# Feed-forward of a two-layer diffusion trunk: gate and up rows by Strassen's seven products, g through HBM, all output products at the end

## The chip, the cores and the metric

One core of one Trainium2 chip runs the whole program in one launch. The metric is the device time of that launch in microseconds (us). Engines are named as in the profile: PE is TensorE's matmuls and PEld its weight loads, DVE is VectorE, ACT is ScalarE, POOL is GpSimd, SP is SyncE, whose queue issues the DMAs.

## What is computed

Two layers over 256 context tokens and 512 latent tokens of width 1024. Each layer is a feed-forward, an attention and a second feed-forward, so there are four feed-forwards, called FFN 0 to FFN 3 here. The last one, FFN 3, has only the 512 latent tokens. What matters of the reference:

```python
def swiglu(h, w_in, w_out):              # w_in (1024, 2 * 2816), w_out (2816, 1024)
    gate, up = jnp.split(h @ w_in, 2, axis=-1)
    return (jax.nn.silu(gate) * up) @ w_out

def half_ffn(h, m, k, g_pre, g_post, w_in, w_out):
    y = swiglu(modulated_norm(h, g_pre, m, k), w_in, w_out)
    return gated_residual(h, y, g_post, m, k, 0.5)
```

## The kernel before

All products are made of fp32r matmuls on split operands: a number x is kept as a high half (a cast to fp32r) and a low half (x minus that), and a product takes three matmuls, high by high, high by low, low by high. `split` (L103) makes the halves: ACT casts (L104) and DVE subtracts (L105). `load_w` loads a weight block of 128 by 1024 into one of four `stage` buffers and splits it into one of six `wh` and six `wl` buffers.

The normed, transposed tokens are the moving operand u, split into `uh` and `ul`: 512 tokens in one tile and 256 in another, each with 8 blocks k of 128 features. `split_u` writes them, DVE and POOL sharing the low half of some tiles (L298, L299).

`ffn` (L424) goes over 22 chunks of 128 hidden features. `w_in` makes gate and up rows of a chunk: two weight blocks, 8 blocks k, 3 matmuls, each over 512 and over 256 tokens (L447): 96 matmuls, or 48 of 512 columns in FFN 3. Then ACT takes silu of gate (L490), DVE multiplies by up to g (L491), casts and subtracts (L501, L502), and g stays on the chip as the stationary operand of the output products. `w_out` adds the output products of a part (pairs of chunks, and six at the end) to `ys`, a tile of 128 tokens at a time, half a row of 1024 at a time (`project_half`, L404; `add_y`, L395). Parts follow each other so that the `w_in` of the next chunk stands in front of the `w_out` of the last part. The first chunk (two of them in FFN 3) runs over pairs of token tiles, 256 columns at a time, since the tokens come in tile by tile from the sub-layer before.

With the last part goes `Finish`: for each token tile the gate multiply on POOL (L350), the norm, the residual (L363), the next norm (L369), transposes on PE (L263), modulation (L277, L273) and the split. In that part the order of DVE, ACT and POOL is the program's (`ordered`); elsewhere in a feed-forward a planner that simulates the engines lays the instructions of every engine out at build time, by priority and by what it holds ready.

Between the products `Fillers` run steps of the conditioning vectors (`ada`): 6, 4, 5 and 1 vectors in FFN 0 to 3, ten steps each, of which eight load 128 by 1024 of weights into a `stage` buffer and make two DVE multiply-adds of 1024 columns (L169, L173).

## Time and profile before

| what | value |
|---|---|
| median of 3 runs | 2843.75 us (2843.62 to 2847.32) |
| the profiled execution: span from first to last instruction | 2845.6 us |
| PE busy | 2766.2 us, 97% |
| DVE busy | 1703.9 us, 60% |
| ACT busy | 908.6 us, 32% |
| POOL busy | 357.7 us, 13% |
| DMA | 291.71 MB, queues 32.3% of 16 engines' span |

A matmul's own duration in the profile is its latency; matmuls are pipelined, so what one costs in a stream is the distance from one start to the next. A group's mean is over all its instructions. "idle before" is the idle time of the engine ahead of an instruction, with what ended it.

### The profile page before, as it was taken

To read this page: it belongs to the slowest core of one execution; us is meant where nothing else is said; L and a number is where in the kernel's file an instruction comes from. 1 tells how busy PE (TensorE), PEld (TensorE's weight loads), DVE (VectorE), ACT (ScalarE), POOL (GpSimd) and SP (SyncE) were. 2 spreads that over 40 slices of the span, in tenths; PEclk is the share of its full clock that TensorE was granted. 3 is DMA by queue.
4 is the path that set the end of the run, shared out by engine and by line. 5 is a ranking of instruction groups with operands and counts; after the bars stand their busy time and mean duration, and the time that the engine had idled before them with its cause. 6 is when DMAs were issued, how large, how long until landed. Compare 5 with 4: busy or idle time off the path is not lost. (4 is left out here: it accounts for less than half of the span.)

```text
span 2845.6 us, 38736 instructions
## 1 busy us (share of the span) xinstructions
PE 2766.2 (97%) x15472; PEld 2399.3 (84%) x15472; DVE 1703.9 (60%) x2516; ACT 908.6 (32%) x1887; POOL 357.7 (13%) x645
## 2 busy tenths in 40 slices
PE   7999999989999989999999999999999899899998
PEld 5888888879999978888888888888888899788887
DVE  5657565367777787456544475556544778755543
ACT  4211111146665564211111232111113554632221
POOL 0000000054333342000000210000002410200001
PEclk9999999999999999999999999999999999999999
DMA  7534334231111115233232243334422211243332
GB/s 239 172 94 146 114 118 136 74 111 44 36 37 41 53 67 174 83 111 122 83 106 89 97 158 104 108 100 128 122 89 97 97 46 53 88 146 111 111 119 74
DMA packets 276812, 291.71 MB, mean 103 GB/s; under 512 B 13032, under 2 KB 231320, under 8 KB 276632
## 3 DMA queue, kind: packets, MB, share of 16 engines
q1 hardware_dynamic: 276632, 289.24, 32.3%
q8 instruction: 121, 1.98, 0.3%
q14 instruction: 59, 0.48, 0.1%
HBM read 272.38 MB, written 16.83 MB: 102 GB/s over the span
## 5 line engine op out<-in xcount | busy, mean ns | idle before, releaser
L447 PE MATMUL ff_ps<-uh,wl 128*128 128x512 f32 (+1 forms) x2544 | 707.8, 342 | 4.2 <-DVE wl L105 4.2
L447 PE MATMUL ff_ps<-uh,wh 128*128 128x512 f32 (+1 forms) x2544 | 704.0, 341 | 5.4 <-ACT uh L1401 3.9
L104 ACT CAST wh<-stage 128x1024 fp32r<-128x1024 f32 x276 | 287.3, 1053 | 1318.1 <-PE ff_ps L447 786.3
L447 PE MATMUL ff_ps<-ul,wh 128*128 128x512 f32 (+1 forms) x2544 | 704.7, 341 | 2.5 <-DVE ul L1402 1.3
L105 DVE TENSOR_TENSOR wl<-stage,wh 128x1024 fp32r<-128x1024 f32 x276 | 333.4, 1220 | 301.2 <-ACT wh L104 301.0
L447 PEld LDWEIGHTS ff_ps<-uh,wh 128*128 128x128 f32 x2544 | 412.0, 189 | 73.0 <-ACT uh L1401 4.0
L447 PEld LDWEIGHTS ff_ps<-uh,wl 128*128 128x128 f32 x2544 | 410.2, 189 | 61.9 <-DVE wl L105 4.6
L447 PEld LDWEIGHTS ff_ps<-ul,wh 128*128 128x128 f32 x2544 | 407.3, 189 | 61.1 <-DVE ul L301 1.8
L395 DVE TENSOR_TENSOR y<-y_ps,y 128x512 f32<-128x512 f32 x412 | 279.7, 688 | 154.3 <-PE y_ps L404 153.2
L404 PE MATMUL y_ps<-wh,g 128*128 128x512 f32 x880 | 344.7, 392 | 0.0
L173 DVE SCALAR_TENSOR_TENSOR acc<-stage,scond,acc 128x1024 f32<-128x1024 f32 x224 | 277.3, 1279 | 50.0 <-DMA stage<-in_ada_w 49.9
L350 POOL TENSOR_TENSOR yg<-y,g 128x512 f32<-128x512 f32 x44 | 57.6, 1309 | 1922.9 <-DVE y L395 1922.9
L491 DVE TENSOR_TENSOR g<-ff_ps,sil 128x768 f32<-128x768 f32 (+2 forms) x89 | 78.4, 881 | 324.4 <-PE ff_ps L447 324.3
L404 PEld LDWEIGHTS y_ps<-wh,g 128*128 128x128 f32 x880 | 165.2, 188 | 36.2 <-DVE y L395 1.6
L404 PE MATMUL y_ps<-wl,g 128*128 128x512 f32 x440 | 171.4, 390 | 0.0
L404 PE MATMUL y_ps<-wl,gh 128*128 128x512 f32 x440 | 171.3, 389 | 0.0
L404 PE MATMUL y_ps<-wh,gh 128*128 128x512 f32 x440 | 171.3, 389 | 0.0
L404 PE MATMUL y_ps<-wh,gl 128*128 128x512 f32 x440 | 171.3, 389 | 0.0
L577 PE MATMUL qkv_ps<-wh,uh 128*128 128x384 f32 x384 | 136.2, 355 | 1.2 <-DVE v L674 1.2
L577 PE MATMUL qkv_ps<-wh,ul 128*128 128x384 f32 x384 | 129.1, 336 | 0.1
L577 PE MATMUL qkv_ps<-wl,uh 128*128 128x384 f32 x384 | 128.8, 335 | 0.0
L404 PE MATMUL y_ps<-wh,ot 128*128 128x512 f32 x320 | 116.2, 415 | 1.2 <-DVE ot L859 0.7
(200 smaller groups left out, 3906.0 us busy)
## 6 DMA issues: line engine op xcount, KB each, us to landing
stage<-in_ffn_w_in SPq DMA_DIRECT2D x176, 512.0 KB
stage<-in_ada_w SPq DMA_DIRECT2D x136, 512.0 KB
stage<-in_ffn_w_out SPq DMA_DIRECT2D x88, 512.0 KB
stage<-in_da_w_in SPq DMA_DIRECT2D x64, 192.0 KB
hd<-h SPq DMA_DIRECT2D x18, 512.0 KB
h<-hd SPq DMA_DIRECT2D x16, 512.0 KB
g<-gd SPq DMA_DIRECT2D x12, 512.0 KB
wl<-hd SPq DMA_DIRECT2D x10, 512.0 KB
```

The costliest lines, as they stand in the source:

```text
L104: nc.scalar.copy(hi, src)
L105: nc.vector.tensor_tensor(out=lo, in0=src, in1=raw(hi), op=ALU.subtract)
L173: nc.vector.scalar_tensor_tensor(out=acc[c], in0=st, scalar=scond[:, k, c : c + 1], in1=acc[c], op0=ALU.mult, op1=ALU.add)
L350: nc.gpsimd.tensor_tensor(out=self.yg[:, cols], in0=ys[t][:, cols], in1=self.gate[1 if t < CT else 0][:, cols], op=ALU.mult)
L395: nc.vector.tensor_tensor(out=y, in0=ps, in1=y, op=ALU.add)
L404: nc.tensor.matmul(ps, lhsT=x, rhs=w, start=(i == 0), stop=(i == n - 1))
L447: nc.tensor.matmul(ps[:, o : o + m], lhsT=ww[:, k, :], rhs=uu[i][:, k, c0 : c0 + m], start=(k == 0 and n == 0), stop=(k == KC - 1 and n == 2),
L491: nc.vector.tensor_tensor(out=of(g), in0=up, in1=of(sil), op=ALU.mult)
L577: nc.tensor.matmul(ps[:, :n], lhsT=x, rhs=w, start=(k == 0 and m == 0), stop=(k == KC - 1 and m == 2))
```

## The change

The tokens are laid out as two halves of 384 (256 in FFN 3): `uh` and `ul` become one tile of (half, k, token) each. A chunk's product [gate; up] by u is taken as a 2 by 2 by 2 block product: gate and up rows, the lower and upper 512 features, the two token halves. It is made of seven products (the form of Strassen's scheme with few additions), each 4 blocks k, 3 matmuls, 384 columns: 84 matmuls a chunk. The first chunk (the first two in FFN 3) stays as it was.

Once per feed-forward, behind the last split of u, four sums of u's blocks are made in `ys` and split. Per chunk, four sums of weight blocks are made on POOL and seven half blocks are split; the sums that undo the scheme are on DVE and POOL. The g of every chunk is stored to HBM. When all chunks are done, g is loaded back in groups, split, and the output products of groups of 2, 3, 3, 3, 3, 3 and 5 chunks follow each other. `operands`, `product`, `chunk`, `operand` and `w_out` are new or rewritten:

```diff
+GROUPS = (2, 3, 3, 3, 3, 3, 5)
-    uh = [res.tile([P, KC, n], F32R, name=f"uh{i}", tag=f"uh{i}") for i, n in enumerate((512, 256))]
+    uh = res.tile([P, 2, KC, HALF], F32R, name="uh", tag="uh")
...
+        seven = range(len(direct), FC)
+        fillers = Fillers(vectors, 2 * len(seven) + 3 * len(GROUPS) - 9, True)
+        gd = [dr.tile([P, nt], F32, name=f"gd{c}", tag=f"gd{c}") for c in range(FC)]
...
+        def keep(c, g):
+            nc.sync.dma_start(out=gd[c], in_=g[:, :nt])
...
+        for m in marks.values():
+            ctx.enter_context(tc.issue_after(m.ins))
...
+        for j, a1, a2, b1, b2 in quarters:
+            nc.vector.tensor_tensor(out=a1, in0=b1, in1=a1, op=ALU.subtract)
+            split_sum(t1, j, a1)
+            nc.gpsimd.tensor_tensor(out=b1, in0=b2, in1=b1, op=ALU.subtract)
+        for j, a1, a2, b1, b2 in quarters:
+            nc.vector.tensor_tensor(out=b2, in0=b2, in1=a1, op=ALU.subtract)
+            split_sum(t2, j, b2)
+            nc.gpsimd.tensor_tensor(out=a2, in0=a2, in1=b2, op=ALU.subtract)
+        for j, a1, a2, b1, b2 in quarters:
+            split_sum(t3, j, b1)
+        for j, a1, a2, b1, b2 in quarters:
+            split_sum(t4, j, a2)
...
+        def operands(c):
+            gate, up = stage(), stage()
...
+            r1, r2 = (xp.tile([P, 1024], F32, tag="raw", name="raw", bufs=2) for _ in range(2))
+            sub = partial(nc.gpsimd.tensor_tensor, op=ALU.subtract)
+            nc.gpsimd.tensor_tensor(out=r1[:, left], in0=up[:, left], in1=up[:, right], op=ALU.add)
+            sub(out=r2[:, left], in0=r1[:, left], in1=gate[:, left])
+            sub(out=r2[:, right], in0=gate[:, left], in1=up[:, left])
+            sub(out=r1[:, right], in0=gate[:, right], in1=r2[:, left])
+            for src in (gate, r1, r2, up[:, right]):
+                hi, lo = wtile("h"), wtile("l")
+                n = src.shape[1]
+                split(hi[:, :n], lo[:, :n], src)
...
+        def product(ps, w, b, first, last):
+            (wh, wl), (bh, bl) = w, b
+            for k in range(4):
+                for n, (ww, bb) in enumerate(((wh, bh), (wh, bl), (wl, bh))):
+                    nc.tensor.matmul(ps[:, :hw], lhsT=ww[:, k * P : (k + 1) * P], rhs=bb[:, k, cols],
...
+        def chunk(c):
+            g1, s1, g2, s4, s2, s3, u2 = operands(c)
+            x, y = bank2("ff_ps"), bank2("ff_ps")
+            pa, pc, pb, pd = x[:, 0], x[:, 1], y[:, 0], y[:, 1]
...
+            product(pa, g1, b11, True, False)
+            nc.scalar.copy(c1, pa[:, :hw])
+            product(pc, s1, t1, True, False)
+            nc.scalar.copy(c5, pc[:, :hw])
+            product(pa, g2, b21, False, True)
+            nc.scalar.activation(sil[:, 0], pa[:, :hw], AF.Silu)
+            fillers.fill()
+            product(pc, s4, b22, False, True)
+            product(pb, s2, t2, True, True)
+            add(out=z2, in0=pb[:, :hw], in1=c1)
+            add(out=sil[:, 1], in0=pc[:, :hw], in1=z2)
+            nc.scalar.activation(sil[:, 1], sil[:, 1], AF.Silu)
+            product(pd, s3, t3, True, False)
+            add(out=z3, in0=pd[:, :hw], in1=z2)
+            nc.gpsimd.tensor_tensor(out=g[:, 1], in0=z3, in1=c5, op=ALU.add)
+            nc.gpsimd.tensor_tensor(out=g[:, 1], in0=g[:, 1], in1=sil[:, 1], op=ALU.mult)
+            product(pd, u2, t4, False, True)
+            add(out=g[:, 0], in0=pd[:, :hw], in1=z2)
+            nc.vector.tensor_tensor(out=g[:, 0], in0=g[:, 0], in1=sil[:, 0], op=ALU.mult)
+            keep(c, g.rearrange("p i n -> p (i n)"))
+            fillers.fill()
...
+        def operand(c):
+            r = stage() if c < GROUPS[0] else ep.tile([P, 768], F32, tag="pl", name="gr", bufs=4)
+            nc.sync.dma_start(out=r[:, :nt], in_=gd[c])
+            gh, gl = two_tiles(next(slots))
+            split(gh[:, :nt], gl[:, :nt], r[:, :nt])
+            w = load_w(w2[c * P : (c + 1) * P, :], (D,))
...
+        for c in seven[:-1]:
+            chunk(c)
+        ops = [operand(c) for c in range(GROUPS[0])]
+        chunk(seven[-1])
+        done = GROUPS[0]
+        for n, size in enumerate(GROUPS[1:]):
+            w_out(ops, n == 0)
+            ops = [operand(c) for c in range(done, done + size)]
+            done += size
+        while fillers.ran < fillers.total:
+            fillers.fill()
+        w_out_last(ops)
```

## Rows read from the trace of the kernel before

**Rows 1.** The page, part 1 (busy us, share, instructions) and PEclk of part 2.
```profile
PE 2766.2 (97%) x15472; PEld 2399.3 (84%) x15472; DVE 1703.9 (60%) x2516; ACT 908.6 (32%) x1887; POOL 357.7 (13%) x645
PEclk9999999999999999999999999999999999999999
```
**Rows 2.** Busy time by stretch, FFN 0, 1, 3: length, PE, PEld, DVE, ACT, POOL.
```profile
100.00:560.00 460.00, 460.00 (x2506) 390.62 (x2505) 258.42 (x292) 79.03 (x87) 0.00 (x0) 1.00 0.37 115
1110.00:1600.00 490.00, 490.00 (x2648) 417.19 (x2647) 249.24 (x280) 86.49 (x95) 0.00 (x0) 1.00 0.34 105
2515.00:2800.00 285.00, 285.00 (x1270) 235.27 (x1269) 144.55 (x178) 67.88 (x78) 0.00 (x0) 1.00 0.38 115
```
**Rows 3.** Chain that ended last, in FFN 3: start us, length us, what.
```profile
2479.54 0.76 DVE y L369
2481.44 12.96 PE ff_ps L447 x108
2510.08 10.88 PE y_ps L404 x48
2520.96 21.76 PE ff_ps L447 x96
```
**Rows 4.** Timeline of PE, twelve matmuls of 384 columns, first and last: start us, us.
```profile
1002.42 0.33 PE L577 MATMUL qkv_ps<-wh,uh 128*128 128x384 f32 x1
...
1004.33 0.34 PE L577 MATMUL qkv_ps<-wh,ul 128*128 128x384 f32 x1
```
**Rows 5.** Groups by form, ACT and DVE: count | busy us, mean ns | idle before.
```profile
L104 ACT CAST wh<-stage 128x1024 fp32r<-128x1024 f32 x276 | 287.3, 1053 | 1318.1 <-PE ff_ps L447 786.3 <-PE y_ps L404 368.8 <-DMA stage<-in_ffn_w_in 114.0
L105 DVE TENSOR_TENSOR wl<-stage,wh 128x1024 fp32r<-128x1024 f32 x276 | 333.4, 1220 | 301.2 <-ACT wh L104 301.0
L502 DVE TENSOR_TENSOR gl<-g,gh 128x512 fp32r<-128x512 f32 x10 | 6.9, 686 | 0.0
L819 DVE TENSOR_TENSOR pt<-p_t,pt 128x384 fp32r<-128x384 f32 x64 | 32.8, 550 | 11.3 <-ACT pt L815 10.9
L819 DVE TENSOR_TENSOR pt<-p_t,pt 128x256 fp32r<-128x256 f32 x16 | 6.7, 417 | 1.1 <-ACT pt L815 0.8
L173 DVE SCALAR_TENSOR_TENSOR acc<-stage,scond,acc 128x1024 f32<-128x1024 f32 x224 | 277.3, 1279 | 50.0 <-DMA stage<-in_ada_w 49.9
```
**Rows 6.** Timelines of DVE and of POOL in the tail of FFN 1: start us, us.
```profile
1639.51 1.79 DVE L298 TENSOR_TENSOR ul<-y,uh 128x512 fp32r<-128x512 f32 x1 [0.30 <-ACT uh L293]
1641.22 1.78 DVE L369 TENSOR_SCALAR y<-h,rms 128x1024 f32<-128x1024 f32 x1
...
1639.46 1.29 POOL L350 TENSOR_TENSOR yg<-y,g 128x512 f32<-128x512 f32 x1
1640.71 1.74 POOL L299 TENSOR_TENSOR ul<-y,uh 128x512 fp32r<-128x512 f32 x1
```
**Rows 7.** Timelines: a DVE instruction alone; POOL with DVE beside it.
```profile
1661.01 0.68 DVE L298 TENSOR_TENSOR ul<-y,uh 128x512 fp32r<-128x512 f32 x1
...
1010.60 0.46 POOL L693 TENSOR_TENSOR q<-c,b 128x128 f32<-128x128 f32 x1
1011.51 2.54 POOL L350 TENSOR_TENSOR wh<-y,g 128x512 f32<-128x512 f32 x2
...
1011.89 0.69 DVE L395 TENSOR_TENSOR y<-y_ps,y 128x512 f32<-128x512 f32 x1 [0.46 <-PE y_ps L404]
```
**Rows 8.** Timeline of PE where an attention ends and FFN 1 begins.
```profile
1079.09 0.41 PE L447 MATMUL ff_ps<-uh,wh 128*128 128x256 f32 x1
1079.31 0.63 PE L404 MATMUL y_ps<-wh,ot 128*128 128x512 f32 x1
```
**Rows 9.** Timeline of PE in the tail of FFN 1, first instruction of a tile's transposes.
```profile
1633.30 1.06 PE L263 MATMUL pre_t<-ident,y 128*128 128x128 f32 x8 [0.59 <-DVE y L369]
```
**Rows 10.** Timeline of DVE at the start of FFN 2, from the last split of u.
```profile
1665.74 1.29 DVE L301 TENSOR_TENSOR ul<-y,uh 128x512 fp32r<-128x512 f32 x2 [1.11 <-ACT uh L293]
1666.95 0.75 DVE L169 TENSOR_SCALAR acc<-stage,scond 128x1024 f32<-128x1024 f32 x1
```

More of the change, by code (lines that the diff above doesn't have):

```diff
@@ L291, in split_u @@
             ks = slice(k, k + n)
[L292 removed]
+            hi, lo = (x[:, i, ks, j * P : (j + 1) * P] for x in (uh, ul))
             marks["act"] = nc.scalar.copy(hi, u32[:, ks])
@@ new lines, in keep, with mms @@
+        def keep(c, g):
+            nc.sync.dma_start(out=gd[c], in_=g[:, :nt])
+        pss = [bank2("ff_ps").rearrange("p i n -> p (i n)") for _ in range(2)]
+        def mms(ps, w, two, ks=range(KC)):
+            wh, wl = w
+            for k in ks:
+                for n, (ww, uu) in enumerate(((wh, uh), (wh, ul), (wl, uh))):
+                    nc.tensor.matmul(
+                        ps,
+                        lhsT=ww[:, k, :],
+                        rhs=moving(uu, k, two),
+                        start=(k == 0 and n == 0),
+                        stop=(k == KC - 1 and n == 2),
+                    )
@@ new lines, in column, with part @@
+        def column(q, n):
+            return slice(512 * q + 256 * n, 512 * q + 256 * n + 256)
+        if opening:
+            second = [bank("ff_ps1") for _ in range(2)]
+            def part(x, w, n, half):
+                ps = second[x][:, :256] if n == 1 else pss[x][:, column(0, n)]
+                mms(ps, w, pairs[n], range(4 * half, 4 * half + 4))
+            opening(part, [ps[:, 512:] for ps in pss])
+        else:
+            ws = [(q, x, early.pop((l, s, c, x), None) or load_in(l, s, c, x)) for q, c in enumerate(direct) for x in range(2)]
+            for n, two in enumerate(pairs):
+                for t in two:
+                    need(t)
+                for m, (q, x, w) in enumerate(ws):
+                    mms(pss[x][:, column(q, n)], w, two)
+                    if two[1] == NT - 3 and m == len(ws) // 2 - 1:
+                        need(NT - 2)
+                        need(NT - 1)
@@ new lines, in ffn @@
+        for m in marks.values():
+            ctx.enter_context(tc.issue_after(m.ins))
+        cols = slice(base, HALF)
+        sums = []
+        for i in range(4):
+            if i == 1:
+                sums.append([x[:, 1, 0:4] for x in (uh, ul)])
+            elif i == 0:
+                sums.append([ep.tile([P, 4, HALF], F32R, tag="v", name="t", bufs=2) for _ in range(2)])
+            else:
+                sums.append([xp.tile([P, 4, HALF], F32R, tag="t", name="t", bufs=4) for _ in range(2)])
@@ new lines, in ffn, with split_sum @@
+        t1, t4, t2, t3 = sums
+        at = {place[t]: t for t in tiles}
+        quarters = []
+        for j in range(base // P, 3):
+            rows = [ys[at[i, j]][:, 512 * k : 512 * k + 512] for i in range(2) for k in range(2)]
+            quarters.append((j, *rows))
+        def split_sum(to, j, src):
+            hi, lo = (x[:, :, j * P : (j + 1) * P] for x in to)
+            src = src.rearrange("p (k q) -> p k q", k=4)
+            nc.scalar.copy(hi, src)
+            nc.vector.tensor_tensor(out=lo, in0=src, in1=raw(hi), op=ALU.subtract)
@@ new lines, in chunk @@
+        def chunk(c):
+            g1, s1, g2, s4, s2, s3, u2 = operands(c)
+            x, y = bank2("ff_ps"), bank2("ff_ps")
+            pa, pc, pb, pd = x[:, 0], x[:, 1], y[:, 0], y[:, 1]
+            one, two, sil, g = (halves(ep.tile([P, 768], F32, tag="pl", name=n, bufs=4)) for n in ("one", "two", "sil", "g"))
+            c1, c5, z2, z3 = one[:, 0], one[:, 1], two[:, 0], two[:, 1]
+            add = partial(nc.vector.tensor_tensor, op=ALU.add)
+            product(pa, g1, b11, True, False)
[19 more added lines that the diff above has]
+            fillers.fill()
@@ L541, in w_out @@
+        def w_out(ops, first):
             for t in tiles:
```

212 lines of the change are left out of this document (83 added, 129 removed).

## The prediction

> **What bounds the kernel now.** I read the page first: PE is busy 97% of the span and the granted clock is at its upper level, 2.4 GHz, in every slice [rows 1]. Then the busy time by stretch: inside a feed-forward PE is busy for the whole of each stretch, while DVE has 51 to 56% and POOL nothing [rows 2], in FFN 2 much the same. So a feed-forward is bound by the number and width of its matmuls, and a change that removes matmul time gains it as long as nobody else becomes late. The chain in order of time gives what a matmul costs in a stream: 108 of 256 columns in 12.96 us, 0.120 each; 96 of 512 columns in 21.76 us, 0.227 each, and output products of 512 the same [rows 3]. For 384 columns the starts of the first and the last of twelve are 1.91 us apart, 0.173 each [rows 4]. The reader should see that these are starts apart; the durations of 0.3 to 0.4 us are latencies.
>
> **Matmuls.** A chunk of 768 tokens has 48 matmuls of 512 and 48 of 256 columns: 48 × (0.2267 + 0.120) = 16.64 us. Seven products of 12 make 84 of 384: 84 × 0.1735 = 14.56. This is 2.08 less, for 21 chunks in each of FFN 0 to 2: 131 us. In FFN 3 a chunk goes from 48 × 0.2267 = 10.88 to 84 × 0.120 = 10.08, 0.80 less for 20 chunks: 16 us. The first chunks and the output products stay. The gain on PE is 147 us; everything else is cost.
>
> **Vector work of a chunk.** Before, POOL did nothing there. Now, with 384 columns a half, DVE makes three low halves of 1024 (1.22) and one of 512 (0.69), four additions from PSUM of 384 (0.55 each, as the row from PSUM) and one multiply of 384 between SBUF tiles (0.55, the nearest row) [rows 5]. POOL makes four sums of 512 and two operations of 384. Two of 512 took 2.54 us, one in the tail 1.29, and one of 128 took 0.46 [rows 6, 7]; between those, 384 is 1.01 and 256 is 0.74. The conditioning's multiply-adds at 1.28 [rows 5] come more densely than before: 42 of the 54 fill points now lie in the 21 chunks. With 96, 64, 80 and 16 of them that is 2 × 96 / 54 = 3.56 a chunk in FFN 0, 2.37 and 2.96 in FFN 1 and 2, and 2 × 16 / 52 = 0.62 in FFN 3.
>
> POOL and DVE do not run freely beside each other. L298, a DVE subtraction of two SBUF tiles, takes 0.68 alone [rows 7] and 1.79 when it starts 0.05 us behind a POOL multiply; the POOL subtraction that starts inside it then takes 1.74 instead of 1.29, and L369 behind that 1.78 [rows 6] instead of 0.76 [rows 3]. The four, 4.02 us alone, needed the time from 1639.46 to 1643.00, 3.54: they ran one after the other, with 12% saved at the hand-overs. An addition from PSUM ran in 0.69 in the middle of POOL's 2.54 [rows 7], so those are free of it.
>
> So what two engines do on two SBUF tiles adds up. Per chunk: DVE 3 × 1.22 + 0.69 + 0.55 = 4.90, POOL 4 × 1.29 + 2 × 1.01 = 7.18, and the multiply-adds: 16.6 us in FFN 0, 15.1 in FFN 1, 15.9 in FFN 2, against PE's 14.56. In FFN 3: 4.77 + 6.64 + 0.79 = 12.2 against 10.08. The excess is 2.08, 0.55, 1.31 (21 times each) and 2.12 (20 times): 125 us. With the 12% saved throughout it is 14.6, 13.3, 14.0 and 10.7: 15 us. If nothing at all overlapped, four additions of 0.55 (0.42 in FFN 3) would come on top: 297 us. I take 70, halfway between 15 and 125: the hand-over saving needs both engines to have work at every moment, and POOL's last two operations wait for PE's sixth product.
>
> The Trainium skill, page "SBUF — State Buffer", section "SBUF: two separate sides", says that DVE and GpSimd share one pair of ports, locked for a whole instruction by a DVE operation with two SBUF inputs or by a GpSimd one, and that the loser fully blocks. The trace agrees (1.79 against 0.68), except for the 12%. By that rule as it stands the term would be 125 instead of 70.
>
> ACT has 3 × 1.05 + 0.6 of casts [rows 5] and four smaller operations of about 0.5: under 6 us a chunk, hidden.
>
> **The wait inside a chunk.** The seventh product adds to the bank of the sixth, so it waits until DVE has read it (z3): 0.16 of the last matmul's latency (0.335 less 0.173), 0.55 of addition and some hand-over, 0.8 us. The planner fills such holes: single matmuls of FFN 1 stand between output products of the attention where those had to wait [rows 8]. The next chunk's first products are free then, so I cost it at nothing; without that cover it is 83 × 0.8 = 66 us, less where the vector work is late anyway.
>
> **The start of a feed-forward.** The sums of u stand behind the last split of u (issue_after) on DVE and ACT, and all of the chunk's weight splits behind that. DVE: 6 sums and 12 low halves of 0.69; POOL: 6 of 1.29; the first weights 4.35 on DVE: 24 us, or 21 with hand-overs. From the last split [rows 10] PE has 48 first-chunk matmuls (5.8 us) and six products (12.5) before it needs the last sum: 18.2. So 3 to 6 us are lost in FFN 1 and 2. FFN 0 has half as many matmuls left: 6 to 9. In FFN 3 two thirds of the sums stand against 20 us of matmuls: nothing. I take 17 in all; 10 to 45 with POOL's weight sums and a multiply-add (which the planner places right there now [rows 10]) in between.
>
> **The tail.** The last output part has five chunks, not six. In the tail PE waits 0.59 us a tile for DVE's next norm, L369 [rows 9], a chain that starts with the first half of a tile's y. The second half covers it with 18 matmuls, now with 15: 0.68 less cover, for five tiles in FFN 0 to 2, 10 us (0 to 14). The fourth and fifth of the last weight blocks wait for buffers of the part before, some 0.6 us, in that.
>
> **At nothing.** g to HBM and back is 64 MB on 292; stores wait on SP for POOL's and DVE's g with the next weight loads queued behind, covered by the four stage buffers; if that cover went, a chunk would wait some 1 to 2 us, the same sign as the vector term. Loads of g in the output part have a group of 16 to 24 us of matmuls to hide in, where DVE needs under 15 and POOL nothing. The removed multiplies, casts and 24 of 108 output additions were hidden already.
>
> **The sum.** 2845.6 − 147 + 70 + 17 + 10 = 2796 for the profiled execution, which is 1.9 above the median of the runs: 2794.
>
> **Rivals.**
> - *The vector work is covered.* Hand-overs save their 12% all the time: 15 instead of 70, 2739. For it: POOL and the weight splits run more than a chunk ahead (six buffers, four a chunk). If only the z3 wait stays uncovered there, 2805, near the forecast by another way.
> - *The ports serialise whole instructions*, the rule as it stands: 125 instead of 70, 2849, no change. For it: each of the two engines is in order, and their pairs rarely meet as in rows 6.
> - *Slower: DVE's queue holds its PSUM additions behind blocked subtractions.* They are free of POOL only when they reach the head of the queue at the right moment, and the next chunk's weight sums wait for two raw buffers that DVE empties. Halfway between 125 and 297, 211: 2935. It ends slower once chunks lose 120 us in all, 1.45 each. For it: PE, DVE and POOL in one loop, and a planner whose order seems not to know of the blocking, since it lays L298 into L350 [rows 6]. Against: DVE is busy only 51 to 56% now [rows 2].
>
> **How the numbers follow.** Forecast 0.42 (its own range 2755 to 2835), covered 0.23, whole-instruction ports 0.13, slower 0.22. The range leaves out about the upper half of the slower case and little of the covered one: 2725 to 2895. About 0.2% (6 us) is what a measurement of this kernel can tell from no change. Faster: 0.42 + 0.23 and a little of the third, 0.66. Same: 0.06. Slower: 0.28.
>
> **What would show it.** In the changed kernel's stretches of products: 384-column matmuls 0.173 apart; POOL busy about half, with DVE's L105 well over 1.22 in the mean; PE below 100% with waits that end at DVE; a chunk at 14.8 to 15.6 us in FFN 0 to 2 and 11.5 in FFN 3. In the output stretches PE near 100%. At each start one wait of some us before the first chunk's later products. Wrong would be: matmuls further apart, PE waiting on DMA in the output part, waits at z3 of 0.8 us in every chunk, or FFN 3 getting faster by 16.

## The result and the profile after

The changed kernel takes 3032.03 us (median of 4 runs, 3026.44 to 3037.15) against 2845.33 for the kernel before beside it: a ratio of 1.0655, 95% interval 1.064 to 1.067. It is slower by 187 us where 50 us of gain were forecast, and it lies outside the range. The profiled execution has a span of 3024.6 us.

The page of the changed kernel, part 1 and PEclk, which answers [rows 1]:

```profile
PE 2728.0 (90%) x15436; PEld 2442.4 (81%) x15436; DVE 2150.1 (71%) x2907; ACT 1212.5 (40%) x2437; POOL 1167.7 (39%) x1165
PEclk8899999999999997999999989999999999999999
```

PE is no longer busy all the time, and four slices of its clock are below the top where none was. The busy time by stretch, for the products of FFN 0, 1 and 3 and for an output stretch of FFN 0 (columns as in [rows 2]):

```profile
100.00:460.00 360.00, 318.99 (x1710) 291.40 (x1711) 276.50 (x263) 112.34 (x160) 198.38 (x115) 0.97 0.46 138
1190.00:1520.00 330.00, 300.59 (x1634) 277.38 (x1633) 231.05 (x226) 109.65 (x156) 172.54 (x114) 0.98 0.42 126
2645.00:2880.00 235.00, 204.15 (x1533) 189.35 (x1533) 160.96 (x178) 94.89 (x148) 142.31 (x106) 0.99 0.40 122
...
480.00:660.00 180.00, 174.64 (x797) 142.36 (x796) 122.17 (x152) 53.04 (x78) 22.37 (x28) 0.99 0.45 149
```

In the products PE is busy 87 to 91%, where it was 100% before [rows 2]; DVE has 68 to 77%, POOL 52 to 61%, so nobody is full. The output stretch has PE at 97%. Most of the loss is in the products; the starts come below.

A chunk is read from ScalarE's copy of its first product (L593) to that of the next. The copies in FFN 1 and in FFN 3 (count, ns min/median/max, first and last start):

```profile
L593 ACT COPY one<-ff_ps x21: 471/480/485, 1179.7 to 1529.7; 128x384 f32<-128x384 f32 x21
...
L593 ACT COPY one<-ff_ps x20: 364/372/373, 2640.4 to 2887.7; 128x256 f32<-128x256 f32 x20
```

That is 350.0 / 20 = 17.50 us and 247.3 / 19 = 13.0 us a chunk, against 14.56 and 10.08 of matmuls and a forecast of 14.8 to 15.6 and 11.5. What ended PE's waits at the products (L576; us, times):

```profile
  DVE two L605: 115.8, 80
  ACT sil L597: 114.9, 131
  DVE g L609: 54.2, 63
  ACT one L593: 32.6, 49
```

L605 is the addition that makes z3, the wait that I had costed at nothing; L597 is the silu of the first half and L609 the chunk's last addition, neither of which I had as a wait. The groups by form that answer [rows 5] and [rows 7]:

```profile
L172 DVE SCALAR_TENSOR_TENSOR acc<-stage,scond,acc 128x1024 f32<-128x1024 f32 x224 | 360.5, 1627 | 64.8 <-DMA stage<-in_ada_w 64.5
...
L104 DVE TENSOR_TENSOR wl<-stage,wh 128x1024 fp32r<-128x1024 f32 x201 | 287.5, 1433 | 46.0 <-ACT wh L103 45.9
L104 DVE TENSOR_TENSOR wl<-raw,wh 128x1024 fp32r<-128x1024 f32 x166 | 214.0, 1291 | 66.8 <-ACT wh L103 66.8
L103 ACT CAST wh<-stage 128x1024 fp32r<-128x1024 f32 x201 | 208.1, 1050 | 368.0 <-PE y_ps L404 268.2 <-PE ff_ps L576 62.9 <-DMA stage<-in_ffn_w_in 15.3
...
L561 POOL TENSOR_TENSOR raw<-stage,raw 128x512 f32<-128x512 f32 x83 | 144.8, 1744 | 1.0
```

The multiply-add takes 1627 ns in the mean instead of 1279 [rows 5], the low half of a staged block 1433 instead of 1220, the GpSimd sum shown 1744 instead of 1.29 us [rows 6] (it is the slowest of the four; the others take 1423, 1476 and 1718). ScalarE's casts keep their 1.05 us. So VectorE and GpSimd do hold each other off, as forecast. Whether that or the waits at the banks cost the time is what the first runs ask.

### The profile page after: what moved, and what is told of

Read it like the earlier page. It is cut to its first block, busy times and chain, and to the rows that moved or that the text cites. A ratio compares the mean times of both kernels' runs of the same rounds, so it can differ in the third digit from the quotient of the medians.

```text
span 3024.6 us, 41430 instructions
## 1 busy us (share of the span) xinstructions
PE 2728.0 (90%) x15436; PEld 2442.4 (81%) x15436; DVE 2150.1 (71%) x2907; ACT 1212.5 (40%) x2437; POOL 1167.7 (39%) x1165
## 5 line engine op out<-in xcount | busy, mean ns | idle before, releaser
L404 PE MATMUL y_ps<-wh,gx 128*128 128x512 f32 x1936 | 605.9, 392 | 0.5 <-ACT y L393 0.5
L576 PE MATMUL ff_ps<-uh,wh 128*128 128x384 f32 (+1 forms) x1328 | 465.7, 351 | 113.4 <-DVE two L605 50.6
L576 PE MATMUL ff_ps<-t,wh 128*128 128x384 f32 (+1 forms) x1992 | 496.5, 332 | 67.8 <-DVE g L609 22.6
L576 PE MATMUL ff_ps<-uh,wl 128*128 128x384 f32 (+1 forms) x1328 | 430.5, 331 | 10.5 <-DVE wl L104 10.5
L576 PE MATMUL ff_ps<-ul,wh 128*128 128x384 f32 (+1 forms) x1328 | 438.7, 330 | 0.0
L404 PEld LDWEIGHTS y_ps<-wh,gx 128*128 128x128 f32 x1936 | 364.8, 188 | 78.3 <-ACT y L393 1.3
L576 PEld LDWEIGHTS ff_ps<-t,wh 128*128 128x128 f32 x1992 | 350.1, 191 | 96.3 <-DVE g L609 31.6
L104 DVE TENSOR_TENSOR wl<-stage,wh 128x1024 fp32r<-128x1024 f32 (+1 forms) x284 | 381.1, 1343 | 46.9 <-ACT wh L103 45.9
L172 DVE SCALAR_TENSOR_TENSOR acc<-stage,scond,acc 128x1024 f32<-128x1024 f32 x224 | 360.5, 1627 | 64.8 <-DMA stage<-in_ada_w 64.5
L576 PEld LDWEIGHTS ff_ps<-uh,wh 128*128 128x128 f32 x1328 | 257.4, 194 | 176.8 <-ACT sil L597 70.4
L404 PE MATMUL y_ps<-wl,gx 128*128 128x512 f32 x968 | 378.4, 391 | 0.0
L576 PE MATMUL ff_ps<-t,wl 128*128 128x384 f32 (+1 forms) x996 | 321.4, 325 | 0.0
L576 PEld LDWEIGHTS ff_ps<-uh,wl 128*128 128x128 f32 x1328 | 256.5, 195 | 11.8 <-DVE wl L104 11.8
L576 PEld LDWEIGHTS ff_ps<-ul,wh 128*128 128x128 f32 x1328 | 258.8, 195 | 0.0
L559 POOL TENSOR_TENSOR raw<-raw,stage 128x512 f32<-128x512 f32 x83 | 118.1, 1423 | 313.3 <-issue 309.9
L558 POOL TENSOR_TENSOR raw<-stage 128x512 f32<-128x512 f32 x83 | 122.5, 1476 | 225.9 <-DMA stage<-in_ffn_w_in 135.4
```

What stands on the lines that cost most here:

```text
L104: nc.vector.tensor_tensor(out=lo, in0=src, in1=raw(hi), op=ALU.subtract)
L172: nc.vector.scalar_tensor_tensor(out=acc[c], in0=st, scalar=scond[:, k, c : c + 1], in1=acc[c], op0=ALU.mult, op1=ALU.add)
L404: nc.tensor.matmul(ps, lhsT=x, rhs=w, start=(i == 0), stop=(i == n - 1))
L558: nc.gpsimd.tensor_tensor(out=r1[:, left], in0=up[:, left], in1=up[:, right], op=ALU.add)
L559: sub(out=r2[:, left], in0=r1[:, left], in1=gate[:, left])
L576: nc.tensor.matmul(ps[:, :hw], lhsT=ww[:, k * P : (k + 1) * P], rhs=bb[:, k, cols], start=(first and k == 0 and n == 0), stop=(last and k ...
```

## The experiments

Mean chunks, in us, from first to last copy as above; the excess is (mean − 14.56) × 20 in FFN 0 to 2 and (mean − 10.08) × 19 in FFN 3, added up. It is not all waiting: where the multiply-adds stand in the products, the conditioning's own few matmuls and, with the bank pairs, some output products stand there too. By the distances of their starts that is some 24 of the changed kernel's 272 us, 11 of e1's 181 and 11 of e6's 47.

| kernel | median | FFN 0 | FFN 1 | FFN 2 | FFN 3 | excess |
|---|---|---|---|---|---|---|
| changed | 3032.0 | 18.64 | 17.50 | 18.33 | 13.01 | 272 |
| e3: no multiply-adds in products | 2991.2 | 16.24 | 16.31 | 16.24 | 12.75 | 153 |
| e1: single banks | 2938.0 | 18.31 | 16.04 | 16.77 | 11.78 | 181 |
| e11: sums on VectorE | 2926.0 | 16.74 | 16.49 | 16.87 | 12.56 | 176 |
| e2: no weight sums | 2898.9 | 16.70 | 16.53 | 16.64 | 11.99 | 160 |
| e8: four single banks, no multiply-adds | 2866.7 | 14.84 | 15.05 | 14.97 | 10.62 | 34 |
| e5: five single banks, no multiply-adds | 2864.0 | 14.78 | 14.93 | 14.82 | 10.57 | 26 |
| e18: single banks, short multiply-adds | 2854.7 | 16.82 | 15.19 | 15.96 | 10.81 | 100 |
| e6: single banks, sums on VectorE | 2800.5 | 15.49 | 15.10 | 15.18 | 10.34 | 47 |

### The banks

**e1, single banks.**

```diff
-            x, y = bank2("ff_ps"), bank2("ff_ps")
-            pa, pc, pb, pd = x[:, 0], x[:, 1], y[:, 0], y[:, 1]
+            pa, pb, pc, pd = (bank("ff_ps") for _ in range(4))
+            pe = bank2("ff_pe")[:, 0]
...
-            product(pd, u2, t4, False, True)
-            add(out=g[:, 0], in0=pd[:, :hw], in1=z2)
+            product(pe, u2, t4, True, True)
+            add(out=g[:, 0], in0=pe[:, :hw], in1=z3)
```

> The five accumulations of a chunk lie in five single banks, so the seventh product no longer adds to the bank that z3 is read from, a chunk's fifth product (s2 t2) no longer shares a pair of banks with the last addition of the chunk before, and a product no longer waits for the read of the other half of its pair. All outputs are computed. Theory W (in-order hand-overs at the banks): PE's waits for z3 (115.8 us in 80), for the silu (114.9 in 131) and for the last addition (54.2 in 63) go, 285 us, less what then waits for something else; I expect 2810 to 2900 us and chunks of 11.0 to 11.8 us in FFN 3 instead of 12.6. Theory P (VectorE and GpSimd one after the other on SBUF set the pace): the waits move to other places, 2990 to 3030 us.

Measured: 2938.04 us, 94 less. The waits for L605 and L609 are gone and that for the silu is 5.5 us; some chunks are at 14.56 us in FFN 0 to 2 and 10.33 in FFN 3, but others take 20 to 25 and one 30, and PE now waits 218.7 us for the copy of the first product. So the banks are a cause and not the only one; theory W's range was missed by 38 us.

**e3, no multiply-adds in the products.**

```diff
-        fillers = Fillers(vectors, 2 * len(seven) + 3 * len(GROUPS) - 9, True)
+        fillers = Fillers(vectors, (len(GROUPS) - 1) * len(pairs), True)
...
-            fillers.fill()
```

The last line goes at both of its places in a chunk.

> The multiply-adds of the conditioning vectors run between output products only, none in the chunks of products. All outputs are computed. Theory F (the densely laid multiply-adds on VectorE are what is late): chunks with one go from 18.7 to the 15.95 us of those without in FFN 1, on three quarters of 63 chunks some 100 us in all, with up to 30 given back in the output stretches, where eight steps stand at one point: 2930 to 2960 us, FFN 3 unchanged. Theories W and P: 15 to 40 us at most, 2990 to 3020 us.

Measured: 2991.20 us, 41 less, in the range of theories W and P. But the chunks did what theory F said: their excess falls by 119 us, and some 73 of it come back in the output stretches, where the multiply-adds now stand (in FFN 0, from the last matmul of the products to the last of the output, 236.5 us instead of 191.7). So 41 us is not what the multiply-adds cost the chunks. Chunks in the body of FFN 0 to 2 are an even 15.95 us, in FFN 3 12.64. This made the wait inside a chunk readable, since each chunk now looks like the one before. In FFN 1, PE and ScalarE (start, us; idle before and its releaser in brackets):

```profile
1302.72 0.34 PE L576 MATMUL ff_ps<-t,wl 128*128 128x384 f32 x1
1303.71 0.45 PE L576 MATMUL ff_ps<-uh,wh 128*128 128x384 f32 x1 [0.66 <-ACT sil L597]
...
1302.22 1.05 ACT L103 CAST wh<-raw 128x1024 fp32r<-128x1024 f32 x1 [2.29 <-PE ff_ps L576]
1303.18 0.48 ACT L597 ACTIVATE sil<-ff_ps 128x384 f32<-128x384 f32 x1
```

The matmul at 1303.71 is the first of the fourth product, s4·b22. It goes to pc and needs nothing of the silu, which reads pa. But pa and pc are two banks of one tile, and the program's waits go by the tile: PE waits until the silu has read pa, and the silu stands in ScalarE's queue behind a cast that itself waited 2.29 us for PE to free a weight buffer. The start is 0.99 us behind the one before it, 0.82 more than in a stream [rows 4]; some smaller gaps of about 0.1 us at the starts of other products make up the rest of 15.95 − 14.56 = 1.39. Over the whole kernel the silu now leads the releasers of PE's waits at the products, and no wait for z3 (L604 there) is among the first ten; L608 is the last addition:

```profile
  ACT sil L597: 130.1, 158
  DVE g L608: 34.0, 40
```

In FFN 3 of the changed kernel the second pair holds a chunk too, where s2·t2 to pb waits for the last addition from pd of the chunk before:

```profile
2733.83 0.50 PE L576 MATMUL ff_ps<-t,wh 128*128 128x256 f32 x2 [0.63 <-DVE g L609]
...
2733.37 0.41 DVE L609 TENSOR_TENSOR g<-ff_ps,two 128x256 f32<-128x256 f32 x1
```

**e5, both edits.** The edits of e1 and of e3.

> The five single banks of the first experiment and the multiply-adds between output products only; all outputs are computed. With the multiply-adds out of the products the chunks ran at an even 15.95 us (FFN 0 to 2) and 12.64 us (FFN 3), in the run with single banks the undisturbed chunks at 14.56 and 10.33. If hand-overs at the banks (W) and the multiply-adds (F) are separate causes, both together give an even 14.56 and 10.33: 60 chunks less 1.39 and 19 less 2.3 us, 127 in all, from 2991 to 2865 us (2845 to 2885). If the single banks only shift the waits to VectorE and GpSimd (P), chunks of 15.5 or more and over 2930 us.

Measured: 2864.04 us, within 1 us of the expectation. The copies of FFN 1 and FFN 3:

```profile
L593 ACT COPY one<-ff_ps x21: 478/483/483, 1150.8 to 1449.4; 128x384 f32<-128x384 f32 x21
...
L593 ACT COPY one<-ff_ps x20: 364/373/374, 2522.3 to 2723.0; 128x256 f32<-128x256 f32 x20
```

298.6 / 20 = 14.93 with the first and the last two chunks, and 14.56 for each of the 17 between, as forecast. In FFN 3 the body is at 10.33 instead of 84 × 0.120 = 10.08. The gain on PE is there.

**e8, z3's wait kept.** As e5, but four single banks and the seventh product adding to pd as in the changed kernel.

> Four single banks, no multiply-adds in the products, but the seventh product again adds to the bank that z3 is read from, so the wait that I costed at nothing is there and the sharing of bank pairs is not. All outputs are computed. If the z3 wait is covered by matmuls of the next chunk, as I put it, chunks run at 14.6 us and 10.4 in FFN 3, and the 1.39 and 2.3 us were the sharing of pairs. If z3's wait is the cause, chunks stay at 15.4 to 16 and 11.2 to 12.6. With both at work, in between, about 15.2 and 11.3.

Measured: 2866.66 us, chunks of 14.61 and 10.37. z3's own wait costs 0.05 us a chunk, since the first matmuls of the next chunk fill it; I had that right. What costs is the sharing of pairs: e3 to e8, with the same number of buffers per bank, is 124.5 us.

**e13, one pair split.**

```diff
-            x, y = bank2("ff_ps"), bank2("ff_ps")
-            pa, pc, pb, pd = x[:, 0], x[:, 1], y[:, 0], y[:, 1]
+            pa, pc, y = bank("ff_ps"), bank("ff_ps"), bank2("ff_ps")
+            pb, pd = y[:, 0], y[:, 1]
```

> No multiply-adds in the products (2991 us, chunks of 15.95 and 12.64), and the first of the two bank pairs split into two single banks; the second pair (fifth to seventh product) stays a pair, now in two buffers. All outputs are computed. If the fourth product waited for the silu only because it shares a pair with the bank that the silu reads, chunks of FFN 0 to 2 go to 14.6 to 14.8 us and the whole to 2865 to 2885. If it is the second pair that holds a chunk, 15.9 us and over 2960.

Measured: 2896.54 us, chunks of 14.73 in the body, 10.49 in FFN 3. With e3's rows, that makes the first pair the cause of the chunk's wait in FFN 0 to 2. The second pair is not cleared by it: this edit gives every bank two buffers, the second pair too, and with one buffer it holds FFN 3, as the rows above show. The whole missed by 11 us: in FFN 0 to 2 the second chunk is 2.0 to 3.2 us longer than in e5, and the last two, where the operands of the first output products are loaded, together 1.3 to 2.2; I did not follow that up.

The Trainium skill, page "Perfetto Trace Analysis", section "Matmuls", says that independent matmul groups should rotate through different PSUM banks, so that reading one out overlaps the next group's matmuls. The trace agrees only where each bank is a tile of its own: different banks of one tile gave 15.95 us a chunk, single ones 14.61.

### VectorE, GpSimd and the multiply-adds

**e2, no weight sums.**

```diff
-            nc.gpsimd.tensor_tensor(out=r1[:, left], in0=up[:, left], in1=up[:, right], op=ALU.add)
-            sub(out=r2[:, left], in0=r1[:, left], in1=gate[:, left])
-            sub(out=r2[:, right], in0=gate[:, left], in1=up[:, left])
-            sub(out=r1[:, right], in0=gate[:, right], in1=r2[:, left])
...
-            for src in (gate, r1, r2, up[:, right]):
+            for src in (gate, up, gate, up[:, right]):
```

> Left out: the four weight sums of a chunk on GpSimd; the halves are made of plain gate and up weights instead, so the feed-forward's values are not those of the reference. VectorE, ScalarE and TensorE have the same instructions as in the changed kernel, GpSimd keeps its two operations on g. Theory P: 83 chunks lose 5.2 us of GpSimd each, and the low halves fall back from 1.29 to 1.34 us to 1.22; FFN 0 to 2 go to 15 us a chunk and the whole to 2800 to 2860 us. Theory W: the order of PE, ScalarE and VectorE is as before and its waits stay; only those that come of longer low halves shrink, 2960 to 3020 us.

Measured: 2898.85 us, 133 less, between the two theories: the shorter chunks of FFN 0 to 2 stand at 15.9, the floor that the pairs set, and but for one of 15.3 none is below it.

**e11, sums on VectorE, and e6, the same with single banks.**

```diff
-            sub = partial(nc.gpsimd.tensor_tensor, op=ALU.subtract)
-            nc.gpsimd.tensor_tensor(out=r1[:, left], in0=up[:, left], in1=up[:, right], op=ALU.add)
+            sub = partial(nc.vector.tensor_tensor, op=ALU.subtract)
+            nc.vector.tensor_tensor(out=r1[:, left], in0=up[:, left], in1=up[:, right], op=ALU.add)
```

> The changed kernel with one edit: the four weight sums of a chunk on VectorE instead of GpSimd; the bank pairs stay. All outputs are computed. Theory P with W: the pairs hold a chunk at 15.95 us at the least (FFN 3 at 11.85), so the sums' locks give back only what lies above that: as with the sums left out, 2898.9, or a little more for 2.7 us of VectorE work: 2895 to 2930. If the sums' locks are the whole of the loss (P alone), 2830 or less; if the sums on GpSimd hurt only together with single banks, over 2990.

> The five single banks; the four weight sums of a chunk on VectorE instead of GpSimd, multiply-adds in the products as in the changed kernel. All outputs are computed. Theory P (each GpSimd sum of 1.29 us holds VectorE's two-tile operations off, and the other way round): VectorE gets 4 x 0.68 = 2.7 us more a chunk and loses 5.2 us of blocking, so chunks of FFN 0 to 2 fall from a mean of 17.0 towards 15.5: 2830 to 2880 us against 2938. If what counts is the length of VectorE's own queue, 2.7 us more in it make the chunks longer: 2960 to 3050 us.

Measured: e11 2926.01 us, e6 2800.52, a ratio of 0.9843 (0.9827 to 0.9859) to the kernel before. e6 beats its expectation. Single banks alone take 94 us off, the sums' move alone 106, both 231.5: each leaves a floor that the other sets. With single banks, 2.7 us a chunk of more work on VectorE's queue makes the kernel 137.5 us faster, so the length of that queue is not what costs.

What the GpSimd sums do is seen in e1, in a chunk of FFN 0 (POOL, ACT, PE):

```profile
198.46 1.40 POOL L558 TENSOR_TENSOR raw<-stage 128x512 f32<-128x512 f32 x1 [6.15 <-DMA stage<-in_ffn_w_in]
...
205.53 1.98 POOL L606 TENSOR_TENSOR g<-two,one 128x384 f32<-128x384 f32 x1
...
207.54 0.48 ACT L593 COPY one<-ff_ps 128x384 f32<-128x384 f32 x1 [0.88 <-POOL g L606]
...
208.07 0.45 PE L576 MATMUL ff_ps<-uh,wh 128*128 128x384 f32 x1 [1.45 <-ACT one L593]
```

Read it from below: PE waits for the copy of the first product, the copy for its buffer (`one`, which the chunk before still holds), the buffer for GpSimd's addition L606. That stands in GpSimd's queue behind four weight sums of a later chunk, and the first of these waited 6.15 us for a late weight load. GpSimd's work ahead and the chunk's own work share one in-order queue.

The load is late partly by GpSimd itself. SyncE's queue from 183 to 195 us, by line of the waiting transfer (us in total, times, longest):

```profile
SPq L554 <- POOL raw L561: 4.9, 1, 4.9
...
SPq L554 <- DVE wl L104: 2.2, 1, 2.2
SPq L554 <- DVE acc L172: 1.9, 1, 1.9
SPq L449 <- POOL g L607: 1.6, 1, 1.6
```

A chunk's first weight load (L554) waits for a low half and then, 4.9 us, until the fourth weight sum of the chunk before (L561) frees a stage buffer; the store of g (L449) behind it waits until GpSimd has made g, and the second load, which the sums need, until a multiply-add frees a buffer. The store's wait for g, which I had put at nothing, is thus part of it here; its share of the whole I did not measure.

**e14, sums doubled, and e16, the same GpSimd work with nobody waiting for it** (both on e5).

```diff
             sub(out=r2[:, left], in0=r1[:, left], in1=gate[:, left])
+            sub(out=r2[:, left], in0=r1[:, left], in1=gate[:, left])
```

In e14 each of the four sums stands twice, as this one; in e16 the sums go as in e2, and there is instead

```diff
+            idle = xp.tile([P, 1024], F32, tag="raw", name="raw", bufs=2)
+            for i in range(8):
+                half = left if i % 2 else right
+                nc.gpsimd.tensor_tensor(out=idle[:, half], in0=gate[:, half], in1=up[:, half], op=ALU.subtract)
```

> Single banks, no multiply-adds in the products (2864 us, chunks of 14.56 and 10.33), and each of the four GpSimd weight sums made twice, the second time with the same result. All outputs are computed. Two-tile work of a chunk is then 4.90 on VectorE and 7.18 + 5.16 = 12.34 on GpSimd. If the two exclude each other for whole instructions, 17.2 us a chunk at least in FFN 0 to 2 (16.2 with GpSimd's 0.74 for 256 columns in FFN 3) and some 3130 us; with 12% saved at every hand-over 15.2 and 14.2, some 2970; if nothing of VectorE's work from PSUM overlaps either, 19.4 and some 3270; if they hardly exclude each other, GpSimd alone is the longest at 12.3 and 11.8, 14.56 stays, and only FFN 3 is slower, 2895.

> Left out: the four weight sums (the halves are made of plain gate and up weights, so the feed-forward's values are not those of the reference). Single banks, no multiply-adds in the products; GpSimd makes eight subtractions of 512 columns a chunk into tiles that nobody reads. VectorE's two-tile work is 4.90 us a chunk, GpSimd's 12.34, TensorE's 14.56. If whole instructions exclude each other and the total is what counts, 17.2 us a chunk in FFN 0 to 2 (16.2 in FFN 3), some 3110 us. If a hand-over saves 0.14 us, as between two rows of the run with doubled sums, on some ten hand-overs a chunk: 15.8 and 14.8, some 3010. If the 16.41 us there were the ring of raw buffers, and exclusion delays single instructions without setting the pace, 14.56 us and, in FFN 3, 12 to 13: 2890 to 2920 us.

Measured: e14 3109.74 us with 16.41 a chunk (15.65 in FFN 3). But GpSimd is not full there; it waits for the raw buffers that VectorE empties, and VectorE is held by GpSimd:

```profile
1345.38 1.29 POOL L558 TENSOR_TENSOR raw<-stage 128x512 f32<-128x512 f32 x1 [1.16 <-DVE wl L104]
1346.75 1.29 POOL L559 TENSOR_TENSOR raw<-stage 128x512 f32<-128x512 f32 x1
...
1347.01 2.11 DVE L104 TENSOR_TENSOR wl<-raw,wh 128x1024 fp32r<-128x1024 f32 x1 [1.71 <-ACT wh L103]
```

The low half starts 0.26 us into a GpSimd sum and ends 1.08 us behind it, which is 0.14 less than its 1.22 alone. So this run gave a ring of waits and not the size. e16 gave it: 3056.42 us, chunks by turns of 14.66 and 16.63, 15.65 in the mean, and 15.0 in FFN 3. GpSimd is never idle there, and its two steps of g, which PE needs, stand in the same queue, so a chunk takes what GpSimd takes. A stretch of FFN 1 (columns as above), and the groups of its subtractions and of VectorE's low halves:

```profile
1300.00:1460.00 160.00, 151.42 (x856) 149.36 (x855) 105.28 (x92) 57.45 (x82) 160.00 (x103) 0.99 0.30 94
```

```profile
L559 POOL TENSOR_TENSOR raw<-stage 128x512 f32<-128x512 f32 x664 | 1087.4, 1670 | 68.7 <-DMA stage<-in_ffn_w_in 67.2 <-DVE h L363 1.5
L104 DVE TENSOR_TENSOR wl<-stage,wh 128x1024 fp32r<-128x1024 f32 x367 | 602.2, 1644 | 347.4 <-ACT wh L103 347.2
```

The two engines' two-tile work is 4.90 + 12.34 = 17.24 us if each runs alone; 15.65 is 9% less, near my 12% of savings. Told from VectorE's side it is less close: GpSimd's 12.34 became 15.65, so of VectorE's 4.90 us 3.31 came on top and a third did not. The whole is 46 us above its expectation, and the starts are some 37 of them (67 instead of 55 us to the first copy in FFN 0, against e5). The Trainium skill, page "SBUF — State Buffer", section "SBUF: two separate sides", has the loser block fully; the trace agrees in the main, but for those 9% of the total.

**e18, short multiply-adds, and e17, three stage buffers.**

e18 is e1 with the first of these edits, e17 is e5 with the second:

```diff
-                        out=acc[c], in0=st, scalar=scond[:, k, c : c + 1], in1=acc[c], op0=ALU.mult, op1=ALU.add
+                        out=acc[c][:, :128], in0=st[:, :128], scalar=scond[:, k, c : c + 1], in1=acc[c][:, :128], op0=ALU.mult, op1=ALU.add
...
-NSTAGE = 4
+NSTAGE = 3
```

> Single banks and the multiply-adds in the products as in the first experiment (2938 us; chunks of 18.3, 16.0, 16.8 and 11.8 us in the mean), but each multiply-add after a vector's first works on 128 of its 1024 columns. Left out: seven eighths of the conditioning products of later vectors, so values are not those of the reference. Loads, buffers and order of the steps stay, some 1.0 of 1.28 us of VectorE goes from each, 3.6 of 4.6 us a chunk in FFN 0. If VectorE's time (by exclusion or by its queue) is what they cost: chunks of 14.6 to 15.2 us, 2830 to 2860 us. If the stage buffers and loads are: chunks of 16 or more stay, 2900 to 2930 us.

> Single banks, no multiply-adds in the products (chunks of 14.56 and 10.33), with three stage buffers instead of four. All outputs are computed. A chunk's two weight loads hold two, so one load of the next chunk can run ahead. If the stage buffers are what the multiply-adds cost the chunks in the run with single banks, chunks go to 16 us or more in FFN 0 to 2; if they have slack, they stay under 15. The attentions and output stretches are slower by both, so only the chunks are read.

Measured: e18 2854.68 us. Its time is in the range of VectorE's time; of its mean chunks FFN 1 is there too (15.19), FFN 0 in that of the loads (16.82) and FFN 2 just below it (15.96). The excess falls from 181 to 100, so about 80 us are VectorE's time, by exclusion or queue. Much of the rest sits in single chunks of 20 to 22 us, where weight loads are late as in e1 (213.2 us of waits for them at the first sum, 256.6 in e1). e17: 2890.17 us, chunks stay at 14.56 in FFN 0 to 2 and go to 11.6 in FFN 3. One stage buffer less is thus no loss by itself in FFN 0 to 2. How much of the loads' lateness is the stage buffers that the multiply-adds hold, and how much the ring through GpSimd's queue shown for e1, stays open; that it needs GpSimd's sums is shown by e6, where the excess is 47.

### The starts and the order

**e4, no sums of u.** The subtractions and splits behind `quarters` go, and four products take plain quarters of u:

```diff
+        t1, t4, t2, t3 = ([x[:, i, k : k + 4] for x in (uh, ul)] for i, k in ((1, 0), (1, 0), (0, 4), (1, 4)))
```

> Left out: the sums of u and their splits at the start of each feed-forward; four products take plain quarters of u instead, so the values are not those of the reference. Theory S (the starts, with TensorE's clock at its lower level of 1.2 GHz in them): the first two chunks of FFN 0 to 2 go from 19 to 26 us to the 16 to 18 of the later ones, and the time at the lower clock falls from 171 us to under 100: 40 to 70 us less, 2960 to 2990 us. If the starts cost what I foresaw, 17 us: 3015. The chunks after the second keep their pace by every theory.

Measured: 2974.22 us, 58 less. From the first matmul of a feed-forward to the first copy it is 38.2, 34.9, 25.0 and 36.9 us instead of 54.9, 50.3, 40.7 and 41.9: 53 us less in the four. The first two chunks did not get shorter (22.5 and 26.9 in FFN 0), against what I expected of theory S, and the time at 1.2 GHz fell to (1 − 0.980) × 2 × 2974 = 119 us, not under 100; the loss lies ahead of those chunks.

**e7, e9, e10: a second direct chunk, and all sums on VectorE.** e7 is e5 and e9 is e6, each with a second direct chunk in FFN 0 to 2; e10 is e9 with GpSimd's share of the sums of u on VectorE.

```diff
+        if nt == NTOK:
+            ws = [load_in(l, s, 1, x) for x in range(2)]
+            more = [[bank("ff_ps2") for _ in range(2)] for _ in range(2)]
+            for n, two in enumerate(pairs):
+                for x, w in enumerate(ws):
+                    mms(more[x][n // 2][:, 256 * (n % 2) : 256 * (n % 2) + 256], w, two)
...
-            nc.gpsimd.tensor_tensor(out=b1, in0=b2, in1=b1, op=ALU.subtract)
+            nc.vector.tensor_tensor(out=b1, in0=b2, in1=b1, op=ALU.subtract)
```

The last edit is e10's; its other GpSimd subtraction, a2, is moved likewise.

> As the run with single banks and no multiply-adds in the products, and FFN 0 to 2 make two chunks of direct products before the seven-product ones instead of one, so that the sums of u stand beside 17 us more of matmuls. All outputs are computed. Theory S: the sums and first weights of a start cost some 15 us in each of FFN 0 to 2; 3 x 12 us less, and 3 x 2.7 us more for a direct chunk in place of a seven-product one: 25 to 30 us less than without the second direct chunk. If the clock's lower level at the starts has another cause, 8 us more than without.

> Single banks, the weight sums on VectorE, the multiply-adds in the products, and a second direct chunk at the starts of FFN 0 to 2. All outputs are computed. The second direct chunk took 31 us off where no multiply-adds stood in the products. If the sums of u are late at the starts here too (theory S), 10 to 30 us less than 2800.5: 2770 to 2790. If the starts are only as long as VectorE's queue there, which the second chunk's four splits lengthen by 5 us each time, 2795 to 2810.

> The same with GpSimd's share of the sums of u on VectorE too, so that GpSimd has nothing at a start. All outputs are computed. Theory P: six GpSimd sums of 1.3 us or more that exclude VectorE become six of 0.69 on it, so each of the starts of FFN 0 to 2 is 3 us shorter: 5 to 12 us less than the run beside it. If the two engines overlap at the starts, VectorE's queue is 4 us longer: 5 to 12 us more.

Measured: e7 2832.76 us, 31 less than e5; e9 2762.62, 38 less than e6; e10 2747.09, another 15.5 less. All three go the way of theories S and P, by more than I expected. Stretches at the start of FFN 0 in the kernel before, in the changed one and in e10 (length, PE, PEld, DVE, ACT, POOL, granted clock):

```profile
72.00:80.00 8.00, 8.00 (x47) 6.97 (x46) 6.88 (x7) 3.19 (x4) 0.00 (x0) 1.00 0.78 258
80.00:88.00 8.00, 8.00 (x48) 6.92 (x47) 8.00 (x9) 0.54 (x1) 0.00 (x0) 1.00 0.78 254
```

```profile
72.00:80.00 8.00, 0.69 (x1) 0.29 (x1) 8.00 (x11) 5.26 (x9) 4.46 (x3) 0.62 0.12 49
80.00:88.00 8.00, 3.77 (x11) 3.38 (x12) 8.00 (x12) 0.73 (x2) 0.00 (x0) 0.50 0.22 63
```

```profile
72.00:80.00 8.00, 8.00 (x69) 8.00 (x69) 8.00 (x16) 4.47 (x9) 0.00 (x0) 1.00 0.01 3
80.00:88.00 8.00, 6.96 (x51) 6.32 (x49) 7.96 (x13) 3.61 (x6) 0.00 (x0) 1.00 0.26 74
```

In the changed kernel VectorE is full for 16 us while PE is busy for 4.5 of them, PE's clock has fallen to its lower level, 1.2 GHz, and the 11 matmuls that come in the second stretch run at that. In e10 PE is busy for 15 of the 16 us and stays at 2.4 GHz.

e10 is the fastest version found: a ratio of 0.9659 (0.9644 to 0.9675) to the kernel before, and it computes all outputs.

**e15, half of the multiply-adds taken out of e10's products.** The point in the middle of a chunk goes (`len(seven) + (len(GROUPS) - 1) * len(pairs)` points in all).

> The fastest version so far (single banks, all sums on VectorE, second direct chunk: 2747 us) with one point for multiply-adds in a chunk instead of two; the steps that go stand in the output stretches. All outputs are computed. If the 0.5 to 1.1 us that its chunks of FFN 0 to 2 take above 14.56 are the multiply-adds', half of them go: 57 chunks less 0.4, 20 to 25 us, of which FFN 0's output stretch gives back up to 15: 2725 to 2745. If they are VectorE's own queue of sums and low halves, no change in the chunks and 2750 to 2760.

Measured: 2749.09 us, no change. Chunks fall by 0.6 and 0.2 us in FFN 0 and 1 and rise by 0.4 in FFN 2 and 0.15 in FFN 3; the output stretches of FFN 0 to 2 give back 2 to 3 us each. Of the 46 us that e10's chunks take above their matmuls, some 11 are the conditioning's own matmuls; the rest I did not settle.

**e12, the order alone.**

```diff
-            product(pa, g1, b11, True, False)
...
+            for x, (wh, wl) in enumerate(ws):
+                for i in range(2):
+                    for k in range(KC):
+                        for n, (ww, uu) in enumerate(((wh, uh), (wh, ul), (wl, uh))):
```

Under these loops stands one matmul of a half of the tokens; the seven products and all sums go.

> The new order without the seven products: every chunk by direct products, 96 matmuls of 384 columns (of 256 in FFN 3), no weight sums and no sums of u, g through HBM, all output products last. All outputs are computed. A chunk is 96 x 0.1735 = 16.66 us, as before; in FFN 3 96 x 0.12 = 11.5 against 10.9, 13 us in all. If the order costs what I put (tail 10, nothing else) 2845 + 13 + 10 = 2868 us (2855 to 2885), and the loss of the changed kernel is the products' alone. If the round trip through HBM or the late output products cost (T), over 2900.

Measured: 2864.97 us, 20.6 above the kernel before; 13 of that are FFN 3's narrower matmuls, so the order, the trip of g through HBM and the shorter last part cost 7.6.

## Why the prediction was wrong

The sum, with what the runs showed for each term:

| term | forecast | measured | from |
|---|---|---|---|
| matmuls | −147 | −147, 5 less in FFN 3 | 14.56 and 10.33 in e5 |
| chunks above their matmuls | +70 | +272 | the copies of the changed kernel |
| starts | +17 | +53 | e4 |
| order and tail | +10 | +8 | e12 |

2845.6 − 147 + 272 + 53 + 8 is 3032, for a span of 3024.6. The 272 hold some 24 us of other matmuls, most of which the kernel before has too, so the terms are good to some 20 us and not to 7. The matmuls were right, and so were order, HBM and tail taken together (e12 does not part them); the two other terms were not.

- **The wait inside a chunk**, put at nothing, is the step whose mechanism failed. I wrote that the seventh product waits for z3, 0.8 us, and that the next chunk's first products are free then. That holds where each bank is a tile of its own: e8 pays 0.05 us. In the changed kernel the banks come in pairs, and I looked at the seventh product alone. s4·b22 waits for the silu of the other half of its pair, and s2·t2 for the last addition of the chunk before. Without multiply-adds this is 1.34 us a chunk in FFN 0 to 2 and 2.27 in FFN 3, 124.5 us in all (e3 to e8); with them, 91 us of excess and 94 of time (the changed kernel to e1, which also drops z3's wait). My upper bound of 66 us was drawn round the wrong wait. In the trace of the changed kernel 115.8 us of waits end at z3, which looked like the price of z3; in e3, with no wait but the pairs', the wait is at the silu. A releaser in a disturbed chunk names the last of several.
- **The vector term** was mis-sized: 70, with bounds of 15 and 125. With single banks, so without the pairs, it is 181 (e1); the slower rival had 211. By estimate some 144 of the 181 are the two engines' work: 26 stay without multiply-adds (e5), and 11 are the conditioning's matmuls. The exclusion of the two engines was put right, in kind and about in size (e16: 9% saved against 12%). Wrong was to compare its mean of 15.1 to 16.6 us a chunk with PE's 14.56 and to charge only the difference. Both engines also carry the chunk's own short steps in the same queues, so in e1 a late weight load holds the copy of the first product, and PE, and chunks come out 6 to 10 us longer, one 15, and others not at all. That the multiply-adds' time is some 80 us of it is shown (e18); by which waits it works in a single chunk is not. Without multiply-adds the same sums cost nothing (e5: 14.56); with the sums on VectorE, though it has 2.7 us more to do, 47.
- **The slower rival** had sign and size (2935, by a term of 211 in place of 70), but not the place: the rows show the short steps behind long work in GpSimd's queue (e1) and ScalarE's (e3), moving the sums took 134 us of excess where shortening the multiply-adds took 81, and with the pairs the chunks' excess is 272.
- **The starts** were 53 us for 17. I let 18 us of matmuls cover 21 to 24 us of VectorE; in the trace PE is busy for 4.5 of 16 us at FFN 0, where the normed tokens come in at the same time. I took FFN 3 at nothing, and it lost 5.
- **The clock** I didn't price. The mean granted clock is 0.972 of the span, against 0.992: (1 − 0.972) × 2 × 3024.6 = 169 us at 1.2 GHz instead of 46. In the stretch of FFN 0 shown above it fell while PE stood idle, so it follows the waits there; e10, with most idle times gone, has 0.989. At half speed 123 us more would be 62 us at the most, a part of the terms above; no run priced it by itself.

## What to carry to other kernels

Where accumulations are read out by another engine while the next run, look at which tile each bank belongs to, not only at which bank: two banks in one tile made a product wait for a reader of the other, 1.3 to 2.3 us a chunk where nothing else disturbed it. And when two engines that exclude each other come near the pace of the one they feed, don't charge the mean: ask for each of their queues which short step of the present chunk stands behind long work for a later one. Moving that long work to the other engine, though its queue got longer, was worth more than any other single edit (137.5 us with single banks, 106 with pairs).

## What I had not expected of the hardware

A cast of 128 by 1024 on ScalarE takes its 1.05 us however VectorE and GpSimd are stretched (1050 ns in the changed kernel, 1053 before). GpSimd work whose results no one waits for slows VectorE as any other does: with the eight free subtractions the low halves took 1644 ns instead of 1220.
